# Stick-breaking attention with one sigmoid a score: the scan keeps the product of what is left

## The chip, the cores and the metric

The kernel runs on one NeuronCore of a Trainium2 chip. The core has a matrix engine (TensorE, PE in the profile; its weight loads are PEld), a vector engine (VectorE, DVE), a scalar engine for table functions (ScalarE, ACT), GpSimd (POOL) and a queue engine (SyncE, SP) that issues DMAs. Each engine works through its own queue of instructions in order; semaphores make one wait for another. The metric is the time of one execution on the device in microseconds (us), the median of several.

## The reference, cut to what matters

The program is a decoder block with three gated attention branches and an MLP. The change lies in the first branch, stick-breaking attention (8 heads of 64, 1024 tokens, 1024 features):

```python
z = einsum(q[q0:kend], k[:kend]) * HD ** -0.5
strict = s_idx < t_idx
log_rem = where(strict, log_sigmoid(-z), 0.0)
after = cumsum(log_rem, axis=3, reverse=True) - log_rem
w = where(strict, exp(log_sigmoid(z) + after), 0.0)
out = einsum(w, v[:kend])
```
In other words: going from the diagonal towards older keys, each key s takes the share beta = sigmoid(z) of what is left of a stick of length one, and 1 - beta = sigmoid(-z) remains for the older ones. With R[s] as what is left after key s, the weight of s is R[s+1] - R[s], and R is 1 on the masked keys. Summed by parts, the output is a sum over s of (1 - R[s]) times a difference of neighbouring values, so it is enough to have R, or 1 - R.

The other two branches are forgetting attention (a softmax with a decay, 8 heads) and attention to 256 memory tokens (4 heads). Gates are a sigmoid of a projection to 3 x 1024.

## The kernel before

All products are made in three passes from operands that are split into a high and a low part (a copy to the matmul type on ScalarE, and a subtraction on VectorE that gives the rest), so most results are followed by such a pair of operations: `whi`/`wlo` for weights (L1054, L1055), `pth`/`ptl` for turned attention weights (L922, L924).

The program runs in this order: norms and first projections (to about 100 us), projections of queries, keys, values and part of the gates by a seven-product scheme (to about 470 us), attention (484 to 876 us), the three branch projections, the output projection, and the MLP, which ends it. Within the attention, the stick-breaking heads come first (4 pairs of heads, 484 to 706 us), then the forgetting heads (4 pairs). Memory attention runs beside them, with the gate projections that are left, and after these the first branch projection.

The order on each engine up to the branch projections is made when the kernel is built, by a small scheduler: each piece of work is a Python generator that asks for places (`Get`) and operations with an estimated cost (`Op`); the scheduler runs them in an estimated time and writes the instructions down in that order. Gate projections and other dense products are "side" work: TensorE takes them whenever no attention operation is ready. So a change of costs or places reorders all the work of the attention stage, while each engine keeps to the written order on the chip, whether or not its estimate holds.

A unit of stick-breaking attention (`unit`, `sb_tile`) is one head and two blocks of 128 queries. Per block and chunk of up to 512 keys: two matmuls make the scores in a PSUM bank (L823, L824); on the chunk with the diagonal VectorE adds the mask to the bank (L834, 128 x 128: 1e30 on masked keys, as the scores are made with -q); ScalarE makes two sigmoids, `rho`, the share that is left (L827), and `beta` into the block's tile `e` or `es` (L828); VectorE scans from the diagonal backwards (L843), x = rho * x + beta, in place on `beta`, which gives 1 - R. `rho` takes one of four places (`RQ`), two halves of each of two tiles `r` of the pool `RR`, lent until the stick-breaking pairs are over; memory attention and the reloads for the branch projections take their tiles from the same pool of three. Then TensorE turns the tile in pieces of 128 x 128 (L917), ScalarE and VectorE make the high and low copies (L922, L924), and four matmuls multiply them with the values (L934). The values were replaced by their neighbours' differences earlier (`value_step`).

The forgetting heads use the same turn, copies and products; their scores are masked and their maxima taken in one VectorE operation (L874), and the exponential is L885. GpSimd makes the mask tile `later` (L1562, L1563) and issues the loads of queries and keys (L1004). For the first branch projection, memory attention's output goes to DRAM and is read back into `r` tiles (L1663, issued by SP) and split (L1054, L1055). The names of tiles carry a running number in the rows of an order.

Of the kernel before, what the change touches and what calls it, by code (L numbers as in the profile page):

```python
# [38 lines left out]
def f32(ap):  # L39
    return ap.bitcast(F32)  # L40
# [3 lines left out]
def tile_hybrid_block(  # L44
# [57 lines left out]
    make_identity(nc, ident)  # L102
    sm = C.p.tile([P, 8], F32, tag="sm", name="sm")
    zero, one = sm[:, 0:1], sm[:, 1:2]
    nc.vector.memset(zero, 0.0)
    nc.vector.memset(one, 1.0)
    gq2, gk2, gmq, gmk, bfg, eps = (sm[:, i:i + 1] for i in range(2, 8))
    nc.vector.memset(eps, EPS * 2.0 ** (2 / 3))
# [178 lines left out]
    def mm_time(*cols):  # L287
        return sum(0.004 + 0.000445 * m for m in cols)
# [61 lines left out]
    PP, SC, TR, PV = (banks(tag) for tag in ("pp", "sc", "tr", "pv"))  # L350
    ES, OO, EL, RR, HT, PH, PL, OB, VV, BK, LATER, NONE, RQ = (Places([]) for _ in range(13))
    SN, RS, S1 = tiles(E, "sn", 10, 512), tiles(R, "raw", 4, 1024), R.t("s1", [P, 4, 256])
# [458 lines left out]

    def sb_tile(pair, b, i, beta):
        n = P * (i + 1)
        q = pair.t["q", b, i // 4][:, (i % 4) * P:(i % 4 + 1) * P]
        ch = chunks(i)
        scanned = Event()

        def chunk(ci, c, m, u):
            rho = yield Get(RQ)
            sc = yield Get(SC)  # L820

            def scores():
                nc.tensor.matmul(sc[:, :m], q, pair.t["k1", b, ci][:, :m], start=True, stop=False)  # L823
                nc.tensor.matmul(sc[:, :m], q, pair.t["k2", b, ci][:, :m], start=False, stop=True)  # L824

            def sigmoids():
                nc.scalar.activation(rho[:, :u], sc[:, :u], AF.Sigmoid, scale=HD ** -0.5)  # L827
                nc.scalar.activation(beta[:, c:c + u], sc[:, :u], AF.Sigmoid, scale=-HD ** -0.5)  # L828

            yield Op("PE", 2 * mm_time(max(m, 256)), scores)  # L830
            last = c + u == n
            if last:
                dg = sc[:, u - P:u]
                yield Op("DVE", 0.22, lambda: nc.vector.tensor_tensor(  # L834
                    dg, dg, holder["later"][:, 385:513], ALU.add))
            yield Op("ACT", act_time(u, u), sigmoids, table=AF.Sigmoid)
            SC.put(sc)
            if not last:
                yield scanned

            def scan():
                back = beta[:, c:c + u][:, ::-1]
                nc.vector.tensor_tensor_scan(out=back, data0=rho[:, :u][:, ::-1], data1=back,  # L843
                                             initial=0.0 if last else beta[:, c + u:c + u + 1],
                                             op0=ALU.mult, op1=ALU.add)
            yield Op("DVE", 0.1 + 0.00215 * u, scan, 0.14)
            RQ.put(rho)
# [40 lines left out]
    def unit(pair, b, g, es):  # L888
# [4 lines left out]
        pair.read(b, g)  # L893
        scr, r0 = o_scr[0 if pair.kind == "sb" else 1], (2 * pair.p + b) * HD
        js = list(range(2 * g + 1, -1, -1))
# [4 lines left out]
        def block(k):  # L900
# [11 lines left out]
            def turn():  # L912
# [8 lines left out]
            ph = yield Get(PH)  # L921
            yield Op("ACT", act_time(512 - lo_c), lambda: nc.scalar.activation(ph[:, lo_c:], tr[:, lo_c:], AF.Copy))  # L922
            pl = yield Get(PL)
            yield Op("DVE", dve_time(512 - lo_c), lambda: nc.vector.tensor_tensor(  # L924
                pl[:, lo_c:], tr[:, lo_c:], f32(ph[:, lo_c:]), ALU.subtract))
            TR.put(tr)
# [633 lines left out]

    def masked(t):
        nc.gpsimd.memset(t, 0.0)  # L1562
        nc.gpsimd.affine_select(out=t[:, 384:], in_=t[:, 384:], pattern=[[-1, P + 1]], compare_op=ALU.is_ge,  # L1563
                                fill=-NEG, base=0, channel_multiplier=1)

    stepped = [Event() for _ in range(2)]

    def value_step(c, g, a, b, more):
        yield Sleep(3.0)
        yield Op("DVE", dve_time(512), lambda: nc.vector.tensor_tensor(a, a, b, ALU.subtract))  # L1570
        ev = yield from put_values(a, f"sb{c}", 2 * g, [b, more])
        SN.put(a)
        yield ev
# [23 lines left out]
    def second_part():  # L1597
        def opened(name, *tags):
            pool = holder[name] = Pool(name, **{tag: n for _, tag, n, _, _ in tags})
            for place, tag, n, shape, dt in tags:  # L1600
# [5 lines left out]
        opened("A", (HT, "h", 12, 512, F32R), (VV, "v", 2, 2048, F32R), (EL, "e", 4, D, F32), (RR, "r", 3, D, F32),  # L1606
               (LATER, "later", 1, 513, F32))
        later = holder["later"] = LATER.free[0]
# [16 lines left out]

    def whole_again(tiles_):
        for pair in pairs[:4]:
            yield pair.over
        RR.put(*tiles_)

# [1090 lines left out]
```

## Time and profile before

| | us |
|---|---|
| median of 3 runs | 1686.24 (1685.2 to 1687.55) |
| span of the profiled execution | 1686.7 |
| ACT busy, and instructions | 848.9, 1474 |
| POOL busy, and instructions | 255.2, 440 |
| DMA: moved over the span | 284.32 MB, 169 GB/s on the mean |
| high and low copies of turned weights, both kinds of head (L922, L924) | 87.4 and 99.1, 160 of each |
| stick-breaking scans (L843) | 66.3 + 26.0, 96 in all |

The span is the time from the first to the last instruction of one profiled execution. "Busy" is the union of an engine's instructions; a row of the groups gives line, engine, operation, output and inputs, shapes, count, busy time, the mean time of one in ns, and the idle time of the engine just before them with what ended it. A busy TensorE may still be held up, since matmuls are pipelined and their ends are modelled; the distance from start to start tells more. An idle engine that nobody waits for costs nothing.

### The profile page before, as it was taken

Reading aid. Unit: us, or ns where it says so; the run is one execution under the profiler, and the core shown is the slowest. Engines: PE = TensorE matmul, PEld = TensorE weight load, DVE = VectorE, ACT = ScalarE, POOL = GpSimd, SP = SyncE. Lnnn points to the kernel's source line nnn. Section 1 sums busy time; section 2 is a strip of 40 time slices with the busy share of each in tenths; the row PEclk is TensorE's granted clock in tenths of the full one; section 3 lists DMA queues with packets and bytes.
Section 4 is the critical chain, followed back from the end, with each engine's and each line's share of the span. In section 5 each row is a group of like instructions: output and inputs, shape, how many; then the busy total and the mean of one; then the engine's idle time right before and its main releaser. Section 6 shows DMA issues by size and latency. Waiting matters only on the chain.

```text
span 1686.7 us, 25003 instructions
## 1 busy us (share of the span) xinstructions
PE 1675.3 (99%) x9118; PEld 1432.0 (85%) x9118; DVE 1293.0 (77%) x2079; ACT 848.9 (50%) x1474; POOL 255.2 (15%) x440
## 2 busy tenths in 40 slices
PE   9999999999999999999999999999999999999999
PEld 9998899998888888888888887878888887888887
DVE  7977778855459888867877898987777776688775
ACT  6455555534358888866761446433333344332331
POOL 0000000000253151254400011022111120000000
PEclk9999999999999999999999999999999999999999
DMA  7445434467475365387747542144444484564532
GB/s 245 157 150 182 149 119 150 146 194 243 127 232 161 111 186 151 117 240 224 236 146 245 183 162 100 57 162 155 152 150 137 150 307 171 202 202 143 198 125 75
DMA packets 142221, 284.32 MB, mean 169 GB/s; under 512 B 16913, under 2 KB 53329, under 8 KB 142098
## 3 DMA queue, kind: packets, MB, share of 16 engines
q1 hardware_dynamic: 110562, 183.08, 32.0%
q0 software_dynamic: 31536, 99.64, 19.5%
q8 instruction: 72, 1.18, 0.3%
q14 instruction: 51, 0.42, 0.1%
HBM read 189.83 MB, written 92.83 MB: 168 GB/s over the span
## 4 chain that ended last, share of the span: by engine, by line
PE 92%; DVE 5%; DMA 2%; ACT 1%; issue 1%; SPq 0%; DVEq 0%; ACTq 0%
PE pp L1456 11%; PE pp L1144 10%; PE pp L1981 10%; PE pp L2658 8%; PE sc L1456 7%; PE sc L1144 6%; PE sc L1981 5%; PE sc L2658 4%; PE tr L2658 4%; PE tr L917 4%; PE pv L1456 3%; PE pv L2658 3%; PE tr L1981 2%; PE sc L934 2%; PE pp L934 2%; DVE h L1917 1%
## 5 line engine op out<-in xcount | busy, mean ns | idle before, releaser
L1055 DVE TENSOR_TENSOR wlo<-raw,whi 128x1024 fp32r<-128x1024 f32 (+1 forms) x88 | 107.5, 1222 | 80.2 <-ACT whi L1054 80.0
L1054 ACT ACTIVATE whi<-raw 128x1024 fp32r<-128x1024 f32 (+1 forms) x88 | 93.2, 1059 | 78.8 <-PE pp L1456 32.7
L2658 PE MATMUL pp<-h,sop 128*128 128x512 f32 x540 | 128.4, 396 | 0.0
L2658 PEld LDWEIGHTS pp<-h,sop 128*128 128x128 f32 x540 | 101.6, 188 | 24.4
L1981 PE MATMUL pp<-h,oh 128*128 128x512 f32 x384 | 121.1, 397 | 0.7 <-ACT cu L2066 0.6
L924 DVE TENSOR_TENSOR ptl<-tr,pth 128x512 fp32r<-128x512 f32 (+1 forms) x160 | 99.1, 628 | 24.1 <-ACT pth L922 23.1
L922 ACT ACTIVATE pth<-tr 128x512 fp32r<-128x512 f32 (+1 forms) x160 | 87.4, 556 | 36.0 <-PE sc L934 15.8
L1981 PEld LDWEIGHTS pp<-h,oh 128*128 128x128 f32 x384 | 72.0, 188 | 19.0 <-ACT cu L2066 1.4
L2573 ACT ACTIVATE h<-t 128x2048 fp32r<-128x2048 f32 (+1 forms) x17 | 30.7, 1814 | 110.2 <-DVE t L1917 97.4
L1373 POOL DMA_DIRECT2D raw<-w_in x32 | 24.2, 755 | 395.1 <-DVE wlo L1055 395.1
L1144 PE MATMUL sc<-h,whi 128*128 128x512 f32 (+1 forms) x254 | 77.7, 389 | 0.0
L1456 PE MATMUL pp<-h,whi 128*128 128x512 f32 x248 | 77.5, 394 | 0.0
L1981 PE MATMUL pp<-h,ol 128*128 128x512 f32 x192 | 76.1, 396 | 0.0
L1456 PE MATMUL pp<-whi,h 128*128 128x256 f32 x384 | 71.8, 283 | 0.0
L843 DVE TENSOR_TENSOR_SCAN e<-r,e 128x384 f32<-128x384 f32 (+3 forms) x64 | 66.3, 1044 | 6.9 <-ACT e L828 6.5
L1974 ACT ACTIVATE oh<-raw 128x512 fp32r<-128x512 f32 x64 | 39.4, 625 | 61.8 <-DVE raw L1917 61.8
L2658 PE MATMUL sc<-h,sop 128*128 128x512 f32 x264 | 63.7, 396 | 0.0
L2658 PE MATMUL tr<-h,sop 128*128 128x512 f32 x264 | 63.4, 396 | 0.0
L1917 DVE TENSOR_TENSOR sop<-ur,sop 128x2048 fp32r<-128x2048 f32 (+1 forms) x28 | 61.8, 2211 | 2.0 <-ACT sop L2586 2.0
L917 PE MATMUL tr<-ident,e 128*128 128x128 f32 x416 | 62.7, 273 | 0.0
L1456 PEld LDWEIGHTS pp<-whi,h 128*128 128x128 f32 x384 | 60.2, 188 | 0.0
L2658 PEld LDWEIGHTS sc<-h,sop 128*128 128x128 f32 x264 | 49.6, 188 | 12.3 <-DVE sop L1917 0.5
(558 smaller groups left out, 5087.7 us busy)
## 6 DMA issues: line engine op xcount, KB each, us to landing
ur<-s_scr SPq DMA_DIRECT2D x26, 1024.0 KB
raw<-w_in POOLq DMA_DIRECT2D x42, 512.0 KB, 4.9
raw<-w_up SPq DMA_DIRECT2D x60, 256.0 KB
s_scr<-s POOLq DMA_DIRECT2D x60, 256.0 KB, 2.7
g<-w_down SPq DMA_DIRECT2D x14, 1024.0 KB
s_scr<-cu POOLq DMA_DIRECT2D x48, 256.0 KB, 2.8
h<-sbk_scr POOLq DMA_DIRECT2D x64, 128.0 KB, 3.2
o<-gate_scr SPq DMA_DIRECT2D x32, 256.0 KB
```

Source lines behind the costliest of these rows:

```text
L843: nc.vector.tensor_tensor_scan(out=back, data0=rho[:, :u][:, ::-1], data1=back, initial=0.0 if last else beta[:, c + u:c + u + 1], op0=ALU ...
L917: nc.tensor.transpose(tr[:, jj * 256 + a * P:jj * 256 + (a + 1) * P], es[a][:, j * P:(j + 1) * P], ident)
L922: yield Op("ACT", act_time(512 - lo_c), lambda: nc.scalar.activation(ph[:, lo_c:], tr[:, lo_c:], AF.Copy))
L924: yield Op("DVE", dve_time(512 - lo_c), lambda: nc.vector.tensor_tensor(pl[:, lo_c:], tr[:, lo_c:], f32(ph[:, lo_c:]), ALU.subtract))
L934: nc.tensor.matmul(pv[0][:, c_:256], pair.v[:, j, b, :], p_[:, jj * 256 + c_:(jj + 1) * 256], start=(k == 0 and n_ == 0 and i == 0), stop= ...
L1054: yield Op("ACT", 0.03 + act_time(m), lambda: nc.scalar.activation(hi, raw, AF.Copy))
L1055: yield Op("DVE", dve_time(m), lambda: nc.vector.tensor_tensor(lo, raw, f32(hi), ALU.subtract))
L1144: nc.tensor.matmul(ps, a_, b_, start=(first and i == 0), stop=(last and i == n - 1))
L1456: nc.tensor.matmul(out_, a_, b_, start=(first and n == 0 and j == 0), stop=(last and n == 3 and j == len(todo) - 1), skip_group_check=True)
L1917: nc.vector.tensor_tensor(out_, a_, b_, op)
L1981: nc.tensor.matmul(ps, w[a_][:, k * P:(k + 1) * P], h[b_][k], start=(first and k == 0 and i == 0), stop=(last and k == 3 and i == 2), skip ...
L2658: nc.tensor.matmul(ps, a_[:, c, qs], b_[:, c, :], start=(kind in ("P1", "P2", "P7") and c == 0 and i == 0), stop=(kind in ("P2", "P4", "P3 ...
```

## The change

The scan keeps the product of what is left, R, instead of 1 - R. Only one sigmoid is made of a chunk's scores, `rho`, straight into the block's tile; the scan multiplies along it in place and takes the larger of the product and a second operand. On the chunk with the diagonal that operand is a tile `floor`, 0 on the keys that count and 1 on the masked ones, so that R stays 1 there; elsewhere it is a column of zeros, spread out. The mask addition in the bank, the tile for `rho` and its places `RQ` go. `floor` takes half of one `r` tile; the other tile that was lent stays in the pool. GpSimd makes two masks (`floor` and `later`, now 512 wide). After the turn, the high copy of a stick-breaking block adds -1 (a function "identity" with a bias column `minus`) and the low copy is (turned - 1) - high; the forgetting heads keep theirs. The differences of values change their sign.

```diff
-    def sb_tile(pair, b, i, beta):
+    def sb_tile(pair, b, i, left):
...
-            rho = yield Get(RQ)
             sc = yield Get(SC)
+            part = left[:, c:c + u]
...
             yield Op("PE", 2 * mm_time(max(m, 256)), scores)
+            yield Op("ACT", act_time(u), lambda: nc.scalar.activation(
+                part, sc[:, :u], AF.Sigmoid, scale=HD ** -0.5), table=AF.Sigmoid)
+            SC.put(sc)
             last = c + u == n
-            if last:
-                dg = sc[:, u - P:u]
-                yield Op("DVE", 0.22, lambda: nc.vector.tensor_tensor(
-                    dg, dg, holder["later"][:, 385:513], ALU.add))
-            yield Op("ACT", act_time(u, u), sigmoids, table=AF.Sigmoid)
-            SC.put(sc)
             if not last:
                 yield scanned
...
+            back = part[:, ::-1]
+            floor = holder["floor"][:, 512 - u:512] if last else zero.to_broadcast([P, u])
+            yield Op("DVE", 0.1 + 0.00215 * u, lambda: nc.vector.tensor_tensor_scan(
+                out=back, data0=back, data1=floor[:, ::-1], initial=1.0 if last else left[:, c + u:c + u + 1],
+                op0=ALU.mult, op1=ALU.max), 0.14)
...
+            yield Op("ACT", act_time(512 - lo_c), lambda: nc.scalar.activation(
+                h_, t_, AF.Identity, bias=minus) if of_sb else nc.scalar.activation(h_, t_, AF.Copy))
...
+            yield Op("DVE", dve_time(512 - lo_c), lambda: nc.vector.scalar_tensor_tensor(
+                pl[:, lo_c:], t_, -1.0, f32(h_), ALU.add, ALU.subtract) if of_sb else nc.vector.tensor_tensor(
+                pl[:, lo_c:], t_, f32(h_), ALU.subtract))
...
-        halves = [RR.free.popleft() for _ in range(2)]
-        RQ.put(*(t[:, i * 512:(i + 1) * 512] for t in halves for i in range(2)))
-        spawn(whole_again(halves))
-        yield Op("POOL", 1.0, lambda: masked(later))
+        lent_ = RR.free.popleft()
+        holder["floor"] = lent_[:, :512]
+        spawn(whole_again(lent_))
+        yield Op("POOL", 1.0, lambda: masked(holder["floor"], 1.0, -1))
+        yield Op("POOL", 1.0, lambda: masked(holder["later"], -NEG, 0))
```

VectorE at the first stick-breaking tiles, before: `pp` is the bank of scores, `r` holds rho, `e` the block's tile, and the scans are the rows of L843.

```order
L834 TENSOR_TENSOR pp_133<-pp_133,later_4697 128x128
L843 SCALAR_TENSOR_TENSOR e_4690<-r_4694,e_4690 128x384
L834 TENSOR_TENSOR pp_133<-pp_133,later_4697 128x128
L843 SCALAR_TENSOR_TENSOR e_4690<-r_4694,e_4690 128x512
L843 SCALAR_TENSOR_TENSOR e_4691<-r_4695,e_4691 128x512
L834 TENSOR_TENSOR pp_133<-pp_133,later_4697 128x128
L843 SCALAR_TENSOR_TENSOR e_4691<-r_4695,e_4691 128x512
L1055 TENSOR_TENSOR wlo_166<-raw_170,whi_165 128x1024
```
The same place in the changed kernel, where L835 is the scan, `r` the floor and `sm` the column of zeros:

```order
L835 SCALAR_TENSOR_TENSOR e_4691<-e_4691,r_4695 128x384
L835 SCALAR_TENSOR_TENSOR e_4691<-e_4691,sm 128x512
L835 SCALAR_TENSOR_TENSOR e_4692<-e_4692,r_4695 128x512
L835 SCALAR_TENSOR_TENSOR e_4693<-e_4693,r_4695 128x128
L835 SCALAR_TENSOR_TENSOR e_4692<-e_4692,sm 128x512
L835 SCALAR_TENSOR_TENSOR e_4693<-e_4693,sm 128x512
L835 SCALAR_TENSOR_TENSOR e_4694<-e_4694,r_4695 128x256
L1049 TENSOR_TENSOR wlo_167<-raw_171,whi_166 128x1024
```
The mask additions are gone and seven scans follow each other where four did, ahead of the same split of a gate's weights.

ScalarE where the first branch projection's operands are split, before. `h` and `whi` are the high parts, `r` the reloaded output of memory attention; `r_4696` is filled a second time behind the first of these rows. `ob` is an output of forgetting attention, `o` a gate.

```order
L1054 ACTIVATE whi_163<-r_4696 128x512
L1054 ACTIVATE h_7212<-r_4694 128x512
L922 ACTIVATE pth_4800<-tr_139 128x384
L1054 ACTIVATE whi_167<-raw_170 128x1024
L1054 ACTIVATE h_7212<-r_4694 128x512
L1054 ACTIVATE h_7213<-r_4695 128x512
L953 ACTIVATE ob_4803<-pp_135 128x256
L953 ACTIVATE ob_4805<-sc_137 128x256
L922 ACTIVATE pth_4799<-tr_138 128x384
L1054 ACTIVATE h_7213<-r_4695 128x512
L922 ACTIVATE pth_4800<-tr_139 128x512
L1054 ACTIVATE h_7214<-r_4696 128x512
```
The same place in the changed kernel (L1048 is the split, L915 the high copy, L947 and L1632 the outputs and gates, L875 the exponential; `r_4697` is the tile that is filled twice):

```order
L1048 ACTIVATE whi_164<-r_4697 128x512
L947 ACTIVATE ob_4804<-sc_138 128x256
L915 ACTIVATE pth_4798<-tr_139 128x384
L915 ACTIVATE pth_4799<-tr_140 128x512
L947 ACTIVATE ob_4802<-pp_136 128x256
L1048 ACTIVATE h_7389<-r_4696 128x512
L1048 ACTIVATE h_7390<-r_4695 128x512
L1632 ACTIVATE o_4810<-pp_135 128x512
L1048 ACTIVATE h_7389<-r_4696 128x512
L1048 ACTIVATE h_7390<-r_4695 128x512
L617 ACTIVATE ob_4803<-tr_139 16x128
L875 ACTIVATE e_4691,fn<-e_4691,st_7393 128x896
```
The row behind it is the split of the refilled tile (`h_7391<-r_4697`). Eleven rows stand between the tile's release and that split where ten stood, and the end of a head pair's outputs and the first exponential of the next pair are now among them.

More of the change, by code (lines that the diff above doesn't have):

```diff
@@ L102, in tile_hybrid_block @@
     make_identity(nc, ident)
-    sm = C.p.tile([P, 8], F32, tag="sm", name="sm")
-    zero, one = sm[:, 0:1], sm[:, 1:2]
+    sm = C.p.tile([P, 9], F32, tag="sm", name="sm")
+    zero, one, minus = sm[:, 0:1], sm[:, 1:2], sm[:, 8:9]
     nc.vector.memset(zero, 0.0)
     nc.vector.memset(one, 1.0)
+    nc.vector.memset(minus, -1.0)
     gq2, gk2, gmq, gmk, bfg, eps = (sm[:, i:i + 1] for i in range(2, 8))
@@ L350, in tile_hybrid_block @@
     PP, SC, TR, PV = (banks(tag) for tag in ("pp", "sc", "tr", "pv"))
-    ES, OO, EL, RR, HT, PH, PL, OB, VV, BK, LATER, NONE, RQ = (Places([]) for _ in range(13))
+    ES, OO, EL, RR, HT, PH, PL, OB, VV, BK, LATER, NONE = (Places([]) for _ in range(12))
     SN, RS, S1 = tiles(E, "sn", 10, 512), tiles(R, "raw", 4, 1024), R.t("s1", [P, 4, 256])
@@ L893, in unit @@
         pair.read(b, g)
-        scr, r0 = o_scr[0 if pair.kind == "sb" else 1], (2 * pair.p + b) * HD
+        of_sb = pair.kind == "sb"
+        scr, r0 = o_scr[0 if of_sb else 1], (2 * pair.p + b) * HD
         js = list(range(2 * g + 1, -1, -1))
@@ L1559, in unit_final, with masked @@
             yield from counted(u, c, spawn(normed_turned(src, ss, hd, {"mq": gmq, "fxk": gk2, "fxq": gq2}[u], out_), 1.0))
-    def masked(t):
+    def masked(t, fill, base):
         nc.gpsimd.memset(t, 0.0)
-        nc.gpsimd.affine_select(out=t[:, 384:], in_=t[:, 384:], pattern=[[-1, P + 1]], compare_op=ALU.is_ge,
-                                fill=-NEG, base=0, channel_multiplier=1)
+        nc.gpsimd.affine_select(out=t[:, 384:], in_=t[:, 384:], pattern=[[-1, P]], compare_op=ALU.is_ge,
+                                fill=fill, base=base, channel_multiplier=1)
     stepped = [Event() for _ in range(2)]
@@ L1624, in second_part, with whole_again @@
         holder["spare"] = pair
-    def whole_again(tiles_):
+    def whole_again(tile_):
         for pair in pairs[:4]:
             yield pair.over
-        RR.put(*tiles_)
+        RR.put(tile_)
     def gate_put(n):
```

20 lines of the change are left out of this document (4 added, 16 removed).

## The prediction

> **What bounds the kernel now.** I read the page's busy shares first, then the table of time windows, then TensorE's waits, then the timeline around the one wait that lies in the changed stage.
>
> ```profile
> span 1686.7 us, 25003 instructions
> PE 1675.3 (99%) x9118; PEld 1432.0 (85%) x9118; DVE 1293.0 (77%) x2079; ACT 848.9 (50%) x1474; POOL 255.2 (15%) x440
> ```
> TensorE is busy in all but 11.4 us. "Busy" on a pipelined engine can hide slack, so the second look is at how fast matmuls follow each other. The columns are the window, its length, then busy time and count for PE, PEld, DVE, ACT, POOL, then the granted clock, DMA share and GB/s.
>
> ```profile
> 250.00:300.00 50.00, 50.00 (x430) 50.00 (x428) 43.52 (x102) 26.42 (x45) 3.17 (x5) 1.00 0.45 140
> 1500.00:1550.00 50.00, 50.00 (x216) 40.32 (x215) 39.03 (x33) 14.88 (x8) 0.00 (x0) 1.00 0.50 172
> 484.00:533.00 49.00, 49.00 (x298) 42.84 (x297) 45.06 (x74) 40.34 (x91) 20.88 (x38) 1.00 0.63 175
> 533.00:572.00 39.00, 39.00 (x252) 34.84 (x251) 34.45 (x64) 32.15 (x74) 8.60 (x14) 1.00 0.49 159
> 572.00:610.00 38.00, 38.00 (x234) 33.39 (x233) 30.79 (x58) 32.82 (x73) 9.19 (x17) 1.00 0.40 114
> 610.00:640.00 30.00, 30.00 (x190) 26.45 (x189) 27.53 (x49) 27.52 (x62) 15.98 (x29) 1.00 0.78 231
> 640.00:670.00 30.00, 30.00 (x190) 26.66 (x189) 26.41 (x48) 25.82 (x55) 4.37 (x7) 1.00 0.34 112
> 670.00:706.00 36.00, 36.00 (x223) 31.54 (x222) 29.16 (x59) 33.11 (x77) 11.55 (x22) 1.00 0.51 147
> 740.00:748.00 8.00, 6.53 (x27) 4.83 (x26) 4.34 (x15) 5.55 (x12) 0.16 (x1) 0.79 0.94 320
> 748.00:862.00 114.00, 114.00 (x761) 101.98 (x760) 95.28 (x266) 83.72 (x198) 47.22 (x87) 1.00 0.70 211
> ```
> The first two rows give prices: a 256-column matmul every 0.116 us (50/430) and a 512-column one every 0.2315 us (50/216).
>
> ```profile
> L824 PE MATMUL pv<-h,h x49: 272/337/398, 484.0 to 703.6; 128*128 128x512 f32 x19, 128*128 128x128 f32 x12, 128*128 128x384 f32 x12, 128*128 128x256 f32 x6
> L824 PE MATMUL pp<-h,h x47: 274/392/402, 483.6 to 694.5; 128*128 128x512 f32 x29, 128*128 128x256 f32 x10, 128*128 128x384 f32 x4, 128*128 128x128 f32 x4
> 712.12 0.44 PE tr L917 x4
> ```
> The last row gives 0.11 us for each of four 128-column transposes. The order of before has 1,367 matmuls from the first to the last stick-breaking score: 534 of 512 columns, 372 of 256, 429 of 128 and 32 of 384 (0.174 by interpolation). At these prices that is 123.6 + 43.3 + 47.2 + 5.6 = 219.7 us. The other two rows, the second matmuls of the scores by the bank they use, put the stretch between 483.6 and 703.6, that is 220.0. So TensorE has no hidden gap in the stick-breaking stage, although DVE is busy 193.4 of its 222 us and ACT 191.8 (sums of the six rows). Both are nearly full, yet neither sets the end: gate products stand between the attention's steps and cover every wait.
>
> **What the change removes.**
>
> ```profile
> L834 DVE TENSOR_TENSOR pv<-pv,later 128x128 f32<-128x128 f32 x38 | 10.9, 287 | 3.9 <-PE pv L824 3.7
> L834 DVE TENSOR_TENSOR pp<-pp,later 128x128 f32<-128x128 f32 x26 | 7.5, 289 | 4.4 <-PE pp L824 4.2
> L827 ACT ACTIVATE r<-pp 128x512 f32<-128x512 f32 (+3 forms) x47 | 24.7, 525 | 8.8 <-DVE pp L834 7.4 <-PE pp L824 0.8 <-DVE pv L834 0.4
> L827 ACT ACTIVATE r<-pv 128x512 f32<-128x512 f32 (+3 forms) x49 | 23.3, 476 | 3.6 <-PE pv L824 2.0 <-DVE pv L834 0.8
> ```
> 64 mask additions leave DVE (10.9 + 7.5 = 18.4 us) and one of two sigmoids leaves ACT in each of 96 chunks (24.7 + 23.3 = 48.0 us). The score bank comes free one sigmoid earlier, and ACT no longer waits for the mask (8.6 us in these rows). All of it lies beside a full TensorE: its worth on the end is **nothing by itself**. TensorE's 9,118 instructions keep their number and shapes.
>
> What moves is their order. In the order of the change the same stretch holds 1,118 matmuls (411, 300, 375 and 32 of the four widths), or 95.1 + 34.9 + 41.3 + 5.6 = 176.9 us. The stage gets some 43 us shorter because fewer gate and memory products are put into it; they come later, among the forgetting attention. That shift costs nothing as long as TensorE stays fed.
>
> **What it adds.** Each scan takes maximum for addition, and has its output as its first operand. No row shows that form, so it is bounded by the nearest: from below by an elementwise pass, from above by the longest whole duration of a present one.
>
> ```profile
> 508.80 1.27 DVE L843 TENSOR_TENSOR_SCAN e<-r,e 128x512 f32<-128x512 f32 x1
> 510.00 0.52 DVE L924 TENSOR_TENSOR ptl<-tr,pth 128x384 fp32r<-128x384 f32 x1
> 510.45 1.20 DVE L843 TENSOR_TENSOR_SCAN e<-r,e 128x512 f32<-128x512 f32 x1
> 511.58 0.65 DVE L924 TENSOR_TENSOR ptl<-tr,pth 128x512 fp32r<-128x512 f32 x1
> 512.16 0.28 DVE L834 TENSOR_TENSOR pv<-pv,later 128x128 f32<-128x128 f32 x1
> 512.36 1.26 DVE L843 TENSOR_TENSOR_SCAN e<-r,e 128x512 f32<-128x512 f32 x1
> ```
> From start to start a 512 scan costs 1.20 and 1.13 us, a 512 low copy 0.58, a 384 one 0.45. A scan in place on its second operand is what these rows already are; I take the same price, 1.18. Ends: 0.58 and 1.27.
>
> The low copy of a turned block gets a third operand, the constant -1, and the high copy a bias read from a column:
>
> ```profile
> L739 DVE SCALAR_TENSOR_TENSOR sn<-tr,sm,sn x26: 737/744/753, 105.8 to 343.3; 128x512 fp32r<-128x512 f32 x26
> L924 DVE TENSOR_TENSOR ptl<-tr,pth 128x512 fp32r<-128x512 f32 x90 | 60.9, 682 | 14.7 <-ACT pth L922 14.0 <-PE pp L824 0.3
> L738 ACT ACTIVATE sn<-tr,sm x26: 670/687/692, 105.1 to 342.4; 128x512 fp32r<-128x512 f32 x26
> L922 ACT ACTIVATE pth<-tr 128x512 fp32r<-128x512 f32 x90 | 53.6, 599 | 11.6 <-PE sc L934 9.2 <-PE pp L934 1.7 <-PE tr L917 0.5
> ```
> The like forms with a column operand take 744 against 682 and 687 against 599. So an added high copy is 0 to 0.09 us dearer (80 of them: at most 7 us on ACT, in the room that 48 us leave), and a low copy 0 to 0.06 us. I take 0.09 and, as a constant needs no column, 0.03.
>
> GpSimd builds a second mask, a fill and a selection:
>
> ```profile
> 429.95 0.55 POOL L1562 MEMSET later<- 128x513 f32 x1
> 430.57 0.29 POOL L1563 TENSOR_SCALAR_AFFINE_SELECT later<-later 128x129 f32<-128x129 f32 x1
> 449.97 0.56 POOL L1004 DMA_DIRECT2D h<-sbk_scr  x1 [19.10 <-DVE wlo L1055]
> ```
> 0.9 us more on POOL. Queued behind it are the first key and query loads, whose reader starts at 484; the queue then waits 19.1 us anyway. Nothing; uncovered it would be 0.9.
>
> **Is VectorE fast enough for the shorter stage?** Counting the change's rows from its first to its last scan: 96 scans (48 of 512, 16 each of 384, 256, 128; each row's mean less 0.07 of overlap) 86 us; 71 low copies 39; output additions, memory softmax and weight splits 31. That is 156 of 177 us, 88%. But over the first 32 scans it is tight: TensorE has 109, 66, 87 and 10 matmuls, 44.3 us; DVE has 29.2 of scans, 9.9 of low copies, 4.6 of the rest, 43.7 us. Before, the same count gives 49.6 of 53.9. At +0.03 on 18 low copies VectorE needs 44.2: just full. I charge **+1.0 us** for waits that then show (ends 0 and 4, the idle that it had there before: 53.9 - 49.6).
>
> **The one wait that can go.**
>
> ```profile
> PE pp L2305 <- ACT h L2280: 1.5, 1, 1.5
> PE pv L869 <- DVE st L874: 1.5, 1, 1.5
> 1020.00:1030.00 10.00, 8.46 (x44) 6.71 (x43) 9.35 (x21) 7.48 (x17) 0.00 (x0) 1.00 0.66 211
> 731.58 8.90 DMA r<-o_scr
> 740.50 0.63 ACT L1054 ACTIVATE h<-r 128x512 fp32r<-128x512 f32 x1 [3.58 <-DMA r<-o_scr]
> 741.17 0.69 DVE L1055 TENSOR_TENSOR h<-r,h 128x512 fp32r<-128x512 f32 x1 [2.32 <-ACT h L1054]
> 742.59 0.50 PE L869 MATMUL pv<-h,h 128*128 128x512 f32 x1 [1.47 <-DVE st L874]
> ```
> At 740 the fourth reload of memory-attention output takes 8.9 us from issue. ACT stands at its split for 3.58 us, DVE behind ACT for 2.32, the maxima behind that keep a score bank, and TensorE stops for 1.5 us. The window 740 to 748 then has a clock of 0.79: another 8 x 0.21 = 1.7 us. In the new order this split stands elsewhere: between the reload's release and DVE's part of the split lie some 10 us of TensorE rows (about 8 before), against 8.9 us of transfer. So I let it go: **-3.2 us**.
>
> The Trainium skill (TensorE: Matmul & The Clock Gate, "HAM oscillation") says that the clock falls when TensorE idles for over some 3.4 us. By that rule this wait costs only its 1.5 us, and the sum would be 1686.2. The trace disagrees at 740 (0.79 after 1.5 us) and agrees at 1020, where 1.5 us left the clock at 1.00. So the 1.7 us depend on where the wait falls.
>
> Sum against the profiled span: 1686.7 - 3.2 + 1.0 = **1684.5 us**. The profiled run lies 0.5 above the median of 1686.24, inside the runs' 1685.2 to 1687.55.
>
> **Rivals.** (1) The wait recurs: the reload still shares the queues with a burst of key loads (DMA share 0.94 in the row of 740), and the split still stands ahead of exponentials and maxima on ACT and DVE. Against it are the 2 us of extra rows. 1686.7, or 1687.7 with the charge. (2) Slower: VectorE cannot keep up in the first 32 scans. It decides from about 0.03 us per low copy upward, or from 2% on the scans; with the full 4 us of idle, or with the 17 scans of 512 columns and the 18 copies at their upper ends (17 x 0.09 + 18 x 0.06 = 2.6), and one spell of low clock (1.7), TensorE loses 4 to 6 us: 1687.5 to 1689.5 with the wait at 740 gone, up to 1692 with it. Against it: at 484 to 533 VectorE was 92% busy and TensorE never waited. (3) The relief of ACT shows at the end after all. For it are ACT's 191.8 busy of 222; against it, TensorE's 219.7 counted in 220.0 measured. At most the 3.2, this 0.3 and no charge: 1683.2. (4) The low clock was not the wait's doing and stays when the wait goes, as the wait at 1020 without one suggests: 1686.7 - 1.5 + 1.0 = 1686.2. The Trainium skill's rule above would have it so.
>
> **How the numbers follow.** Forecast, 0.43: wait gone, small charge, 1683.5 to 1686. Wait recurs, 0.17: 1686 to 1688. Low clock stays, 0.06: 1685.5 to 1687. VectorE lags, 0.22: 1687.5 to 1692. No charge at all, 0.12: 1682.5 to 1683.5. Medians lie 0.5 under these, so the range reaches from 1682 to 1691 and leaves out only the ends of the first and last cases. A measurement of this kernel tells about 0.2%, 3.4 us, from no change: under 1682.9 or over 1689.6. Faster is the no-charge case and a sixth of the forecast (its lower edge): 0.12 + 0.07 = 0.19. Slower is three quarters of the VectorE case: 0.17. Within: 0.64.
>
> **What would show it.** Right: the page keeps PE at 99% with 9,118 matmuls; the last score stands near 661 (484 + 177) instead of 704; ACT loses about 48 us less the added bias; no TensorE wait for L874's successor near the first branch product. Wrong: TensorE waits on transposes or score banks between 484 and 530, scans above 1.3 us per 512 columns, a clock under 1 in a window before 700, or a span under 1682.

## The result, and the profile after

| | median us | lowest to highest | runs |
|---|---|---|---|
| before | 1685.73 | 1684.96 to 1688.06 | 20 |
| changed | 1688.62 | 1687.97 to 1690.24 | 20 |

The ratio is 1.0015, with a 95% interval of 1.0009 to 1.0022: the changed kernel is slower by 0.09 to 0.22%, some 2.5 us (2.9 between the medians), where it was forecast 2.2 us under the profiled span. The time lies inside the range given, but on the other side of no change.

The page of the changed kernel, whose profiled execution has a span of 1688.5 us (1690.24 us of device time):

```profile
span 1688.5 us, 24767 instructions
...
PE 1677.8 (99%) x9118; PEld 1432.9 (85%) x9118; DVE 1279.1 (76%) x2016; ACT 817.4 (48%) x1374; POOL 256.7 (15%) x442
...
PEclk9999999999999999999999999999999999999999
```
TensorE has its 9,118 matmuls still, ScalarE and VectorE have less to do, and no slice of the span has a low clock. Yet TensorE is busy 2.5 us longer (1677.8 against 1675.3). The windows, in the columns of the prediction:

```profile
250.00:300.00 50.00, 50.00 (x427) 50.00 (x427) 43.19 (x100) 27.27 (x47) 2.99 (x4) 1.00 0.48 149
1500.00:1550.00 50.00, 50.00 (x215) 40.20 (x214) 38.89 (x33) 14.88 (x8) 0.00 (x0) 1.00 0.51 174
484.00:533.00 49.00, 49.00 (x297) 42.83 (x296) 42.28 (x57) 32.55 (x64) 22.32 (x41) 1.00 0.62 182
640.00:670.00 30.00, 30.00 (x189) 26.32 (x188) 26.05 (x38) 19.44 (x38) 14.77 (x27) 1.00 0.75 235
740.00:748.00 8.00, 7.31 (x36) 5.83 (x35) 2.83 (x6) 2.95 (x6) 3.30 (x7) 1.00 1.04 315
```
The first two rows are the ones to look at twice. At 250 the same code now starts 427 matmuls in 50 us instead of 430, and at 1500 215 instead of 216, far from anything that the change edits. A count in a window is too coarse for this; the first and last start of a group of matmuls that both kernels have is not. Three such groups, their line, count, shortest, median and longest duration in ns, then first and last start; the changed kernel:

```profile
L1450 PE MATMUL pp<-h,whi x248: 387/394/401, 116.6 to 481.8; 128*128 128x512 f32 x124
L1976 PE MATMUL pp<-h,oh x384: 391/394/500, 1071.0 to 1366.8; 128*128 128x512 f32 x192
L2653 PE MATMUL pp<-h,sop x540: 392/397/401, 1391.9 to 1681.2; 128*128 128x512 f32 x180
```
and the kernel before, in the profile of the prediction:

```profile
L1456 PE MATMUL pp<-h,whi x248: 388/394/401, 115.7 to 480.2; 128*128 128x512 f32 x124
L1981 PE MATMUL pp<-h,oh x384: 392/396/504, 1070.9 to 1366.0; 128*128 128x512 f32 x192
L2658 PE MATMUL pp<-h,sop x540: 392/394/399, 1391.1 to 1679.5; 128*128 128x512 f32 x180
```
The first group ends before the attention, the second begins behind it, the third is the last stage. So the changed kernel is 1.6 us late when the attention begins (481.8 against 480.2), makes good 1.5 us in it (from the one start to the other 589.2 against 590.7), and then loses 0.7 us from 1071 to 1367 (295.8 against 295.1) and 0.9 us in the last stage (289.3 against 288.4). The parts that the change does not edit lose. What the edited part seems to gain stands against this one execution of the kernel before, which holds the wait at 740; a second one (s1 below) takes 588.0 us there, less than the 589.2 of the changed kernel. In the last stage 1,235 matmuls lie between the two starts: 234.3 ns each, against 233.5.

What can differ where the code is the same? The addresses, through the column `minus`. `sm` had 8 columns of 4 bytes and now has 9, tiles are laid out in steps of 32 bytes, and the tiles that are allocated behind `sm` on the left side of SBUF (the on-chip memory that the engines read) stand 32 bytes further on: in bytes within a partition, as the program's allocation lists them, the first `sop` at 42816 instead of 42784. The right side's tiles (`h`, `g` and `x` of the last stage, `mt`, `sn`) stay. So do the few behind `later` (`pth` and `ptl` among them), as `later` is a column shorter. The edit of `sm` has one line in the diff and no term in the prediction.

### The profile page after: what moved, and what is told of

Read it like the earlier page. It is cut to its first block, busy times and chain, and to the rows that moved or that the text cites. A ratio compares the mean times of both kernels' runs of the same rounds, so it can differ in the third digit from the quotient of the medians.

```text
span 1688.5 us, 24767 instructions
## 1 busy us (share of the span) xinstructions
PE 1677.8 (99%) x9118; PEld 1432.9 (85%) x9118; DVE 1279.1 (76%) x2016; ACT 817.4 (48%) x1374; POOL 256.7 (15%) x442
## 4 chain that ended last, share of the span: by engine, by line
PE 91%; DVE 4%; DMA 3%; ACT 1%; issue 1%; SPq 0%; DVEq 0%; ACTq 0%
PE pp L1450 11%; PE pp L1976 10%; PE pp L1138 10%; PE pp L2653 8%; PE sc L1450 7%; PE sc L1138 6%; PE sc L1976 5%; PE sc L2653 4%; PE tr L2653 4%; PE tr L908 4%; PE pv L1450 3%; PE pv L2653 3%; PE tr L1976 2%; PE pp L928 2%; PE sc L928 2%; DMA raw<-w_in 1%
## 5 line engine op out<-in xcount | busy, mean ns | idle before, releaser
L1048 ACT ACTIVATE whi<-raw 128x1024 fp32r<-128x1024 f32 (+1 forms) x88 | 93.1, 1058 | 82.5 <-PE pp L1450 32.8
L918 DVE TENSOR_TENSOR ptl<-tr,pth 128x384 fp32r<-128x384 f32 (+1 forms) x80 | 50.3, 634 | 24.0 <-ACT pth L915 23.8
L914 ACT ACTIVATE pth<-tr,sm 128x384 fp32r<-128x384 f32 (+1 forms) x80 | 50.7, 647 | 23.7 <-PE sc L928 11.0
L917 DVE SCALAR_TENSOR_TENSOR ptl<-tr,pth 128x384 fp32r<-128x384 f32 (+1 forms) x80 | 49.3, 622 | 14.2 <-ACT pth L914 13.7
```

Of the source, the lines that this page charges most:

```text
L917: yield Op("DVE", dve_time(512 - lo_c), lambda: nc.vector.scalar_tensor_tensor(pl[:, lo_c:], t_, -1.0, f32(h_), ALU.add, ALU.subtract) if ...
L918: pl[:, lo_c:], t_, -1.0, f32(h_), ALU.add, ALU.subtract) if of_sb else nc.vector.tensor_tensor(
L1048: yield Op("ACT", 0.03 + act_time(m), lambda: nc.scalar.activation(hi, raw, AF.Copy))
```

## The experiments

The theories: **T1**, the 32 bytes slow the matmuls and the change itself gains or is even. **T2**, the new order or the new operations cost it, and addresses do not matter. **T3**, the two kernels do not differ. Runs are named by group and number (r1, r2, and so on).

**First group.** r1, the change again, as it is.

> The changed kernel once more, as the reference of this group. Theory T1 (addresses): the new ninth column of sm moves every tile that is allocated after it on the left side of SBUF by 32 bytes, and matmuls on moved operands follow each other some 0.2 to 0.4% more slowly; that costs about 3 us over the whole program and hides a gain of 1 to 3 us in the changed stage. T2 (order and operations): the new order, the scan or the copies cost it, addresses do not matter. T3: the two kernels do not differ, the difference came from one chip. T1 and T2 expect a ratio of 1.001 to 1.002 to the kernel before, T3 expects 1.000. In the trace T1 expects the first 3,000 matmuls, which are the same in both kernels, to end about 1.4 us later than before.

Measured: 1688.83 us, ratio 1.0015 (1.0007 to 1.0024). The result stands; T3 falls. The first group of matmuls ends at 481.0, 0.8 us later than in the profile of the prediction, where T1 had some 1.4.

r2, the change with the addresses of before (`later` keeps its 513 columns too):

```diff
-    sm = C.p.tile([P, 9], F32, tag="sm", name="sm")
+    sm = C.p.tile([P, 8], F32, tag="sm", name="sm")
...
+        holder["minus"] = lent_[:, 512:513]
         yield Op("POOL", 1.0, lambda: masked(holder["floor"], 1.0, -1))
+        yield Op("POOL", 0.5, lambda: nc.gpsimd.memset(holder["minus"], -1.0))
```


> The whole change, but sm keeps its 8 columns, so that every tile keeps the address that it has before the change; the column of -1 stands in the free half of the tile that the floor borrows, and one small fill on GpSimd is added. T1: the unchanged parts run at the speed of before, and what the reordering gains shows: 0.998 to 0.9995, some 1683 to 1685. T2: as the change itself, 1.001 to 1.002.

Measured: 1696.85 us, 1.0066 (1.0053 to 1.0078), worse than anything expected. But the added step made the scheduler write down another order for the attention, so the time of this run is no test of addresses. Its last stage is one: the group there takes 288.1 us (1399.3 to 1687.4), about the 288.4 of before and not the 289.3 of the change. Where the run loses its time there is a wait of the kind that the prediction had at 740. The windows of this run, around the place where it falls behind:

```profile
770.00:780.00 10.00, 9.52 (x64) 8.14 (x63) 5.51 (x9) 6.07 (x13) 3.25 (x7) 1.00 1.01 337
780.00:790.00 10.00, 7.24 (x22) 5.73 (x23) 4.41 (x10) 3.68 (x8) 4.67 (x9) 0.67 1.06 320
790.00:800.00 10.00, 8.47 (x51) 6.64 (x49) 7.80 (x26) 7.00 (x16) 2.08 (x4) 0.99 0.64 185
```
and its timeline there (start, duration, engine, line, and in brackets the idle time ahead and what ended it):

```profile
780.20 0.40 PE L1137 MATMUL sc<-h,wlo 128*128 128x512 f32 x1
...
781.87 0.63 ACT L1047 ACTIVATE h<-r 128x512 fp32r<-128x512 f32 x1 [1.72 <-DMA r<-o_scr]
782.41 0.96 ACT L914 ACTIVATE pth<-tr 128x384 fp32r<-128x384 f32 x2
...
782.93 0.39 PE L927 MATMUL sc<-pth,v 128*128 128x256 f32 x1 [2.33 <-ACT pth L914]
```
A late reload holds ScalarE, the high copies queue behind it, TensorE stops for 2.33 us, and the granted clock falls to 0.67. Only 22 matmuls start in those 10 us.

r3, the kernel before with `sm` wider, the added column never used:

```diff
-    sm = C.p.tile([P, 8], F32, tag="sm", name="sm")
+    sm = C.p.tile([P, 9], F32, tag="sm", name="sm")
```


> The kernel before with one edit: sm has 9 columns in place of 8, the ninth is never used, and all tiles behind it on the left side stand 32 bytes further on. T1: slower by some 3 us, 1.0015 to 1.003 (the change's loss with none of its gain). T2 and T3: 1.000, within 0.0005.

Measured: 1688.45 us, 1.0014 (1.0005 to 1.0022). One unused column, in a kernel that has nothing else of the change, costs all that the change costs. Its rows of the three groups:

```profile
L1456 PE MATMUL pp<-h,whi x248: 387/394/401, 115.8 to 481.0; 128*128 128x512 f32 x124
L1981 PE MATMUL pp<-h,oh x384: 391/395/501, 1069.2 to 1365.0; 128*128 128x512 f32 x192
L2658 PE MATMUL pp<-h,sop x540: 392/397/401, 1390.1 to 1679.4; 128*128 128x512 f32 x180
```
The last stage takes 289.3 us and the one from 1069 on 295.8, as in the changed kernel. T1 holds, T2 falls.

r4, the same with `[P, 17]`:

> The kernel before with sm of 17 columns, so that the tiles behind it stand 64 bytes further on. If T1 holds and what matters is the place within 64 bytes: 1.000, within 0.0005. If any move of 32 bytes or more costs (distance to the tiles on the right side, or place within 128 bytes): 1.001 to 1.003. T2 and T3: 1.000.

Measured: 1686.17 us, 0.9999 (0.9990 to 1.0009): 64 bytes cost nothing.

**Second group.** s1, the kernel before, unchanged, for a second look at the wait at 740.

> The kernel before, profiled once more. The prediction's largest term, -3.2 us, is a wait of 1.5 us at 740 with a low clock behind it, read from one profile whose run took 1687.55 us, the highest of its three. If the wait belongs to the order of before (as predicted): it stands here again, 1.5 us and a clock near 0.8 in the window of 740 to 748. If it was the luck of that one execution: no such wait, clock 1.00, and a span near 1684.5. Time 1.000 either way.

(The 1687.55 in this text was my assumption; the time of the execution that was profiled before is not on record.) Measured: 1686.01 us, and this execution has a span of 1683.5. Its window of 740, TensorE's wait there (total, times, longest, in us), and the transfer on its chain (start, duration):

```profile
740.00:748.00 8.00, 7.77 (x46) 6.23 (x45) 5.93 (x23) 6.52 (x15) 2.11 (x4) 1.00 0.94 331
```
```profile
PE pv L869 <- DVE st L874: 0.2, 1, 0.2
```
```profile
731.45 7.67 DMA r<-o_scr
```
The same reload lands after 7.67 us instead of 8.90, TensorE waits 0.2 instead of 1.5, the clock stays at 1.00, and 46 matmuls start in those 8 us instead of 27. So the wait's length and the low clock belonged to one execution. The profiles of the kernel before with moved tiles agree: at this place TensorE waits 0.5 us in s4, 0.6 in t1, 1.0 in u4 and not at all in r3 and r4, with the clock at 1.00 each time. In the three groups s1 has:

```profile
L1456 PE MATMUL pp<-h,whi x248: 388/394/401, 115.6 to 480.0; 128*128 128x512 f32 x124
L1981 PE MATMUL pp<-h,oh x384: 393/396/504, 1068.0 to 1363.1; 128*128 128x512 f32 x192
L2658 PE MATMUL pp<-h,sop x540: 394/394/394, 1388.2 to 1676.4; 128*128 128x512 f32 x180
```
From the first group's end to the second's start are 588.0 us, 2.7 less than in the profile of the prediction.

s2, the change with the addresses of before, in its own order:

```diff
+        def lent_filled():
+            masked(holder["floor"], 1.0, -1)
+            nc.gpsimd.memset(holder["minus"], -1.0)
-        yield Op("POOL", 1.0, lambda: masked(holder["floor"], 1.0, -1))
+        yield Op("POOL", 1.0, lent_filled)
```
(with `sm` of 8 columns, `later` of 513 and `minus` as in r2)

> The whole change with the tile addresses of before, and this time in the very order of the change: the column of -1 is filled inside the step that makes the floor, so no step is added. T1 (addresses cost it all, the change itself brings 0 to +0.5 us): 0.9995 to 1.0005, some 1686. T2 (order or operations): 1.001 to 1.002. If the extra 8 us of r2_change_old_addresses came from the old addresses and not from its added step: 1.006.

Measured: 1685.47 us, 0.9998 (0.9989 to 1.0007).

```profile
L1449 PE MATMUL pp<-h,whi x248: 388/394/401, 115.6 to 480.1; 128*128 128x512 f32 x124
L1980 PE MATMUL pp<-h,oh x384: 388/394/503, 1067.3 to 1362.5; 128*128 128x512 f32 x192
L2657 PE MATMUL pp<-h,sop x540: 394/394/394, 1387.5 to 1675.7; 128*128 128x512 f32 x180
```
With the addresses the rate of the unedited parts is back (480.1, 295.2 and 288.2, against 480.0, 295.1 and 288.2), and between them the change is 0.8 us shorter (587.2 against 588.0). So the 8 us by which r2 lies over r1 came from its added step.

s3, the change with `sm` of `[P, 17]`:

> The change with sm of 17 columns instead of 9: every tile behind it 64 bytes from where it is before, the order that of the change. T1, by r4_before_plus64 (64 bytes cost nothing) and the 0.4 us between r1 and r3: 0.9995 to 1.0005. T2: 1.0015, as the change.

Measured: 1685.44 us, 0.9996 (0.9987 to 1.0005).

s4, the kernel before with the right side moved:

```diff
+    PAD = Pool("pad", side="right", pad=1)
+    PAD.t("pad", [P, 8])
     RA = Pool("ra", side="right", h=4, g0=1, g1=1, g2=1, g3=1)
```


> The kernel before; the left side stays, and an unused pad of 32 bytes moves all tiles of the right side down by 32. If what costs is how a matmul's two operands, one on the left and one on the right, stand to each other: as r3_before_plus32, 1.001 to 1.002. If it is the place of the left tiles alone: 1.000. If it is the place of each operand by itself, the right side's tiles pay or gain too: any value but 1.000, with other groups of matmuls slower than in r3.

Measured: 1689.94 us, 1.0020 (1.0011 to 1.0030), with 289.4 us in the last stage's group. Moving the other operand costs as well.

**Third group.** t1, two moves of the kernel before together: `sm` of 9 columns (r3) and the pad (s4).

> The kernel before with both moves: the left side's tiles 32 bytes up, as in r3_before_plus32, and the right side's 32 bytes down, as in s4_before_right32, so that the two sides stand to each other as before within 64 bytes, while each is elsewhere. If the two operands' places to each other count: the last stage's matmuls (one operand on each side) return to the rate of before, about 0.43% under that of the two runs, and the time is 0.9995 to 1.0005. If each side's own place counts, the two losses (1.0014 and 1.002) add up: 1.003 to 1.004.

Measured: 1686.45 us, 0.9999 (0.9990 to 1.0008). Two losses add up to none. The last stage's group in s4 and in t1:

```profile
L2660 PE MATMUL pp<-h,sop x540: 392/397/400, 1392.6 to 1682.0; 128*128 128x512 f32 x180
```
```profile
L2660 PE MATMUL pp<-h,sop x540: 387/394/398, 1388.8 to 1676.9; 128*128 128x512 f32 x180
```
289.4 against 288.1 us. What counts in the last stage is where the two operands of a matmul stand **to each other**.

Is VectorE as full as the prediction had it? t2, the change of s3 with its first 18 low copies made twice:

```diff
+                    holder["lows"] = holder.get("lows", 0) + 1
+                    for _ in range(2 if holder["lows"] <= 18 else 1):
+                        nc.vector.scalar_tensor_tensor(pl[:, lo_c:], t_, -1.0, f32(h_), ALU.add, ALU.subtract)
```


> The change as in s3_change_plus64 (its addresses cost nothing), with one edit: each of the first 18 low copies of the stick-breaking stage is issued twice in a row, with the same result, 18 times about 0.55 us, some 10 us, of added work on VectorE; nothing else moves. As the prediction had it (VectorE has 43.7 us of work against 44.3 of TensorE over the first 32 scans, just full): TensorE waits for nearly all of it, 8 to 10 us, 1.005 to 1.006, with waits on low copies or score banks between 484 and 533. Theory now (VectorE runs some microseconds ahead and its idle time, 6.6 us in that window of s3, takes a part, gate products in between the rest): under 5 us, 1.000 to 1.003.

Measured: 1693.91 us, 1.0047 (1.0034 to 1.0061), 8.5 us over s3 (1685.44). Its TensorE waits, and its first window of the stage:

```profile
PE tr L908 <- DVE ptl L922: 3.0, 6, 0.8
PE pp L934 <- DVE ptl L922: 2.2, 4, 1.0
```
```profile
484.00:533.00 49.00, 44.89 (x254) 36.69 (x252) 44.23 (x62) 27.66 (x54) 21.05 (x39) 1.00 0.62 173
```
254 matmuls start where 297 did. In this trace the second of two copies starts 0.71 us behind the first on the mean of the 11 pairs of 512 columns and 0.57 us on that of the 7 pairs of 384, so the added work is 11 x 0.71 + 7 x 0.57 = 11.8 us, and only some 3 us of it were covered. The prediction's "just full" is nearly right; the theory that I held against it here is not.

t3, the change of s2 with a pad for the late stages alone:

```diff
+    LATE = Pool("late", pad=1)
+    LATE.t("pad", [P, 16])
     M = Pool("m", raw=8, oh=8, ol=8, cu=8)
```


> The change with the addresses of before, as in s2_change_plus0, and one unused pad of 64 bytes on the left side, opened only for the stages after the attention (the tiles oh, ol, cu and raw). From the traces of r4_before_plus64 the matmuls of 1070 to 1350 run about 0.4% faster with these tiles 64 bytes further on, those before 480 are faster with the old addresses; together they should give some 1 us less than s2_change_plus0: 0.9985 to 0.9995 to the kernel before. If the tiles of those stages that this pad does not move (whi, h) are what counted: as s2, 0.9998.

Measured: 1683.59 us, 0.9985 (0.9976 to 0.9994), with 293.9 us in the second group, against 295.2 in s2: at the lower edge of what was expected, 1.9 us under s2 where some 1 was forecast.

t4, the change with `sm` of `[P, 33]`:

> The change with sm of 33 columns: every tile behind it 128 bytes from where it is before, the order that of the change. If only the place within 64 bytes counts: as s2 and s3, 0.9995 to 1.0005, with the stage of 1070 to 1350 like one or the other. If the pattern repeats every 128 bytes: that stage as in s2 (297.3 us in the same 1,200 matmuls) and not as in s3 (296.0).

Measured: 1675.98 us, 0.9943 (0.9929 to 0.9956). Nobody expected this: 10 us less than before, and neither of the two patterns.

**Fourth group**, to see the rule. u1, u2 and u3, the change with `[P, 49]`, `[P, 41]` and `[P, 25]`, and u4, the kernel before with `[P, 33]`.

> The change with sm of 49 columns: the left side's tiles 192 bytes from where they are before. In the last stage the moving operand (right side) and the stationary one (left side) stand 192 bytes apart within 256 before the change; matmuls of 512 columns followed each other there every 233.3 ns at a distance of 192, 234.3 at 160, 233.3 at 128, 228.9 at 64 (t4). Here the distance is 0, as it is for those matmuls of that stage whose two operands lie on one side, which took 226.7 to 227. T5 (the distance within 256 bytes sets the rate): 226.7 to 228 in the last stage, 1670 to 1675 in all, 0.990 to 0.9935. T6 (128 bytes was a lucky place, no rule by distance): 1676 to 1690.

> The change with sm of 41 columns, 160 bytes: distance 32 in the last stage. T5: between the distances 64 and 0, 226.7 to 229.5 ns, 1671 to 1677, 0.991 to 0.995. T6, or if 32-byte steps are worse by themselves, as at the change's own place: 1680 to 1690.

> The change with sm of 25 columns, 96 bytes: distance 96 in the last stage. T5: between the distances 128 (233.3 ns) and 64 (228.9), 229 to 234 ns, 1676 to 1686, 0.994 to 1.000. If an odd multiple of 32 bytes is worse than its neighbours: 1686 to 1690.

> The kernel before with sm of 33 columns, the layout of t4_change_plus128. If the gain of t4 is the layout's alone: 0.9940 to 0.9950, 1676 to 1677, at most 1 us over t4. If the change has part in it: above 0.9955.

All the moves, in one table. The distance is the address of the moving operand (`h`) less that of the stationary one (`sop`) in the last stage, within 256 bytes; the last column is the span of the third group, in the runs of the change, over its 1,235 matmuls.

| left side moved by | distance | kernel before, us | change, us | ratio of the change | ns a matmul, last stage |
|---|---|---|---|---|---|
| 0 | 192 | 1686.01 (s1) | 1685.47 (s2) | 0.9998 (0.9989 to 1.0007) | 233.4 |
| 32 | 160 | 1688.45 (r3) | 1688.83 (r1) | 1.0015 (1.0007 to 1.0024) | 234.3 |
| 64 | 128 | 1686.17 (r4) | 1685.44 (s3) | 0.9996 (0.9987 to 1.0005) | 233.4 |
| 96 | 96 | | 1687.08 (u3) | 1.0006 (0.9997 to 1.0015) | 233.4 |
| 128 | 64 | 1677.15 (u4) | 1675.98 (t4) | 0.9943 (0.9929 to 0.9956) | 228.8 |
| 160 | 32 | | 1685.89 (u2) | 1.0000 (0.9991 to 1.0009) | 233.3 |
| 192 | 0 | | 1670.31 (u1) | 0.9906 (0.9893 to 0.9920) | 226.7 |

The rows of the last stage in u1 and in u2:

```profile
L2653 PE MATMUL pp<-h,sop x540: 388/389/398, 1381.4 to 1661.4; 128*128 128x512 f32 x180
```
```profile
L2653 PE MATMUL pp<-h,sop x540: 393/396/399, 1389.2 to 1677.3; 128*128 128x512 f32 x180
```
280.0 us against 288.1. u1 is as T5 has it, and it beats the kernel before by 0.9% and the change by 1.1%. u2 falls between its two neighbours in distance but not in time (1671 to 1677 expected): T5's smooth rule by distance is wrong. In total time the three odd multiples of 32 are slower than the even ones on either side of them (u3's 1687.08 is what its text has for that case), and of the even ones a distance of 0 is best and 64 next. u4 has the gain of t4 without the change (0.9946, 0.9932 to 0.9959), so it is the layout's; the change brings 1.2 us there, a little over the 1 us expected.

The distances of 0 and 64 were reached by moving the left side only. Is it then the place of `sop` by itself? The kernel before answers for 0: 48 matmuls of the last stage multiply `sop` with `sop`, 0 apart, with every tile where it always stood. In s1:

```profile
L2658 PE MATMUL sc<-sop,sop x24: 387/389/398, 1377.3 to 1382.5; 128*128 128x512 f32 x24
L2658 PE MATMUL tr<-sop,sop x24: 389/389/389, 1382.7 to 1388.0; 128*128 128x512 f32 x24
```
From the first start to the last these are 47 steps in 10.7 us, 228 ns each, where the group of `h` and `sop` right behind them takes 233.4. So `sop` need not move for the quick rate.

## Why the prediction was wrong, point by point

- **The step that failed** is the sentence that "TensorE's 9,118 instructions keep their number and shapes", used as if they therefore kept their pace. The added column moved one side's tiles by 32 bytes. That is worth +2.4 us by itself (r3 less s1, 1688.45 - 1686.01), and the change at unmoved addresses is even (s2). The sum had no term for it, nor had any rival. The measured time lies inside the rival of a lagging VectorE (1687.5 to 1692) and near that of a wait that recurs (1687.7); that is luck. VectorE never held TensorE between 484 and 533, and of the wait only 0.7 us came back.
- **-3.2 us for the wait at 740** had about the right price and the wrong baseline. The price: the profile of the prediction lost 2.7 us against s1 between the same two matmuls. But a second profile of the same kernel waits 0.2 us there with a full clock, and five more with moved tiles wait 0 to 1.0 us, so the median can have held little of those 3.2 us. The claim that the profiled run lay 0.5 above the median compared a span with a device time; in the later runs the device time is 1.7 to 1.8 above the span (1690.24 and 1688.5 in the changed kernel, 1685.31 and 1683.5 in s1), so by my estimate a span of 1686.7 was an execution of some 1688.4, two over the median. Nor did the wait vanish: in the changed kernel the reload takes 10.38 us and TensorE waits, a little later, with the clock at 1.00. Chain and waits of the changed kernel:

```profile
729.95 10.38 DMA r<-o_scr
```
```profile
PE pv L859 <- DVE st L864: 0.7, 1, 0.7
```
- **+1.0 us for a VectorE that is just full**: not seen, TensorE has no wait between 484 and 533 (49.00 of 49.00). The low copies became no dearer, which the charge rested on, while the high copies cost the 0.09 us forecast (647 against 553 ns). The changed kernel's low copies (L917 and L918) and high copies (L914 and L915), stick-breaking first, forgetting second:

```profile
L917 DVE SCALAR_TENSOR_TENSOR ptl<-tr,pth 128x384 fp32r<-128x384 f32 (+1 forms) x80 | 49.3, 622 | 14.2 <-ACT pth L914 13.7
L918 DVE TENSOR_TENSOR ptl<-tr,pth 128x384 fp32r<-128x384 f32 (+1 forms) x80 | 50.3, 634 | 24.0 <-ACT pth L915 23.8
L914 ACT ACTIVATE pth<-tr,sm 128x384 fp32r<-128x384 f32 (+1 forms) x80 | 50.7, 647 | 23.7 <-PE sc L928 11.0
L915 ACT ACTIVATE pth<-tr 128x384 fp32r<-128x384 f32 (+1 forms) x80 | 43.5, 553 | 29.5 <-PE pp L928 13.4 <-PE sc L928 10.0 <-PE tr L908 5.7
```
  How near the edge lies was roughly right (t2): by the 3 us that t2 covered, an estimate, the rival of a lagging VectorE decides from about 3 / 18 = 0.2 us a low copy, not 0.03.
- **Scans**: as costed. The 512-column scan in place takes 1.27 us from start to end, as much as the longest of the prediction's rows:

```profile
L835 DVE TENSOR_TENSOR_SCAN e<-e,sm 128x512 f32<-128x512 f32 x32 | 40.6, 1272 | 2.7 <-ACT e L827 1.9
```
- **The stage shortens and pays nothing for it**: right. The last score stands at 664 (661 forecast, 704 before):

```profile
L825 PE MATMUL pp<-h,h x51: 273/337/400, 486.6 to 664.2; 128*128 128x512 f32 x21, 128*128 128x128 f32 x11, 128*128 128x384 f32 x10, 128*128 128x256 f32 x9
```
- **Work that leaves ScalarE and VectorE** is worth next to nothing: right. The page shows 31.5 us less on ScalarE (forecast 48.0, less at most 7 for the bias) and 13.9 on VectorE (forecast 18.4). The forecast added up groups, in which instructions that overlap are both counted in full; the page's busy time is their union.
- **What the change itself brings**, from equal layouts: -0.5 (s2 and s1), +0.4 (r1 and r3), -0.7 (s3 and r4), -1.2 (t4 and u4). Their mean, -0.5 us, can't be told from nothing with intervals of some 0.1% (1.5 us) either way. Only s2 and s1 have every tile in the same place; in the other three pairs the tiles behind `later` differ by 32 bytes.

**What stays open.** Why the places of the operands count. The Trainium skill (SBUF — State Buffer, "A bandwidth-pool intuition that's wrong (but worth ruling out)") gives TensorE a second, independent read port for weight loads, from which I would have expected that the place of the weights to the moving data does not matter. The runs speak against that expectation: 226.7 to 234.3 ns for the same 1,235 matmuls. That the weight load collides with the moving read is a guess; it was not tried by itself. Between 0 and 32 bytes, and beyond 192, nothing was tried either. Nor is the distance the whole rule outside the last stage. In the stage from 1071 on, 64 matmuls multiply `whi` with `oh`, both on the left side and 0 apart. In s1, and in s4, which moves neither of the two, they read:

```profile
L1981 PE MATMUL sc<-whi,oh x64: 388/397/398, 1070.8 to 1348.9; 128*128 128x512 f32 x64
```
```profile
L1983 PE MATMUL sc<-whi,oh x64: 388/389/398, 1074.9 to 1353.2; 128*128 128x512 f32 x64
```
The next matmul starts 235.5 ns behind one of them on the mean in s1 and 228.7 in s4, so something besides these two addresses counts there.

## What to carry to other kernels

An edit that changes the size of a small tile moves every tile behind it; where TensorE sets the time, compare the kernels with the addresses held equal before you credit or blame the edit, and try a few pads as an optimisation of its own (0.9% here, for 160 unused bytes). Look at the same matmuls in the parts that the change does not touch: if they drift, the cause is global. And profile twice before you price a wait: one execution's wait need not be in the median.

## What the hardware showed that was not expected

- In the last stage, matmuls of 512 columns, with no wait in sight and a granted clock of 1.00, followed each other every 226.7, 228.8, 233.4 or 234.3 ns, by the distance of their operands' addresses (0, 64, 192 and 160 within 256 bytes). The busy column shows nothing of it: the window of 1500 to 1550 reads 50.00 of 50.00 in both kernels.
- The granted clock fell to 0.67 over 10 us behind a stop of 2.33 us (r2). The Trainium skill (TensorE: Matmul & The Clock Gate, "HAM oscillation") lets it fall after idling of over some 3.4 us. The runs disagree here as at 740 in the prediction; a stop of 0.7 us at 747 (changed kernel) left it at 1.00. The length of a stop alone does not decide it: in r2 one of 2.18 us at 1033 left the clock at 1.00 over the 10 us around it (1030 to 1040).
- One more half-microsecond step in the scheduler's list, 0.5 us on an engine with 85% idle time, cost 11 us (r2 less s2, 1696.85 - 1685.47) through the order that it led to.
